# Weight sums and a running sum of squares: the same subtractions and additions on GpSimd instead of VectorE

## The chip, the cores and the metric

The kernel runs on one core of a Trainium2 chip. The core has a matrix engine (TensorE, PE in the profile, with its weight loads as PEld), a vector engine (VectorE, DVE), an activation engine (ScalarE, ACT), GpSimd (POOL) and SyncE (SP), which here issues the DMA transfers. Each engine works through its own instruction stream in order and waits at semaphores for the others. The metric is the device time of one execution in microseconds.

## The reference, cut to what matters

One layer of an encoder: 2048 tokens of width 1024, all in float32.

```
xn   = RMSNorm(x)
proj = xn @ w_in                      # attention q,k,v; mLSTM q,k,v,o and gates; ga, gm
A    = chunked band attention with a relative-position bias, 8 heads of 64
M    = mLSTM in chunks of 64, 4 heads of 128, with convolution, norm and output gate
y    = sigmoid(ga) * (A @ w_att_proj) + sigmoid(gm) * (M @ w_mlstm_proj)
x    = x + y @ w_out
x    = x + relu(RMSNorm(x) @ w_up)^2 @ w_down
out  = RMSNorm(x)
```

## The kernel before, in words

**Tiling.** Tokens are cut into four blocks of 512. Every float32 product is made of three TensorE passes in a rounded format (fp32r): each operand is split into a rounded upper part, which ScalarE copies, and the remainder, which VectorE subtracts (L427 and L429 for weights of 128x1024, L963 and L968 for activations of 128x512); then come high times high, high times low and low times high. A DMA puts raw weights into one of four buffers `wraw`, the split weights lie in one of three buffers `wsp`.

**Seven products for eight.** The output projection, both feed-forward matrices and the input projection of blocks 2 and 3 work on a matrix of two by two quarters with seven products instead of eight (`quad`, L571, and `quad_tok`, L599). This needs sums of quarters on both sides. For weights some sums are formed once ahead of time and kept in DRAM as `wsum` (`self.td`): `sum_w(q)` at L381 loads the four quarters of half a quad, 128x512 each, from `in_wf` into four buffers of the pool `ctx` (L391), forms `c-a`, `d-c`, `d-(c-a)` and `b-(d-(c-a))` in place (L396), and after each sends the result to DRAM (`store`, L2054). The third subtraction overwrites the first one's result, so it waits until that has been stored. Fourteen quads with two halves of four subtractions make 112. The loader later reads the sums as weights (L409, `wraw<-wsum`). Other sums are formed when the weights are first used (`quad_w`, L446).

The results of the seven products are put together by `combine`: ScalarE copies a bank to `ctx` (L1764), VectorE adds the next bank to it (L1772), and that sets the bank free for the next product.

**The squares.** `norm_mid` (L2059) needs, for the norm ahead of the feed-forward part, the sum of squares of the residual stream over the 1024 features of a block. `square_mid` (L2084) loads one of eight tiles of 128x512 into a buffer `sc`, ScalarE squares it (L2089), and for all but the first VectorE adds it to a running sum in a buffer `bias` (L2093). Four blocks with seven additions make 28. The result is needed much later, when the feed-forward output is added to the residual stream (`residual`, L2141).

**What sets the order.** The instruction streams are written by a planner (`Flow`, L95) when the program is built. Every piece of work is a thread that names an engine and an assumed duration (`yield "dve", dve_ns(512)`), waits for events and takes buffers from pools; `run` (L173) picks what can start first by its own clock, then by priority. Its choice fixes the order on each engine, on SP's queue of DMA issues, and which buffer is taken. The times assumed there are not those of the chip, and the chip follows only the order and the semaphores.

**Stages.** Up to about 640 us blocks 0 and 1 go through the input projection, attention and the recurrence. To about 1500 us follow gate and output products, the input products of blocks 2 and 3 (with most weight sums beside them) and the first up-projection. To about 2150 us the attention and recurrence of blocks 2 and 3 run beside the first down-projection; then comes the same tail for blocks 2 and 3.

Of the kernel before, what the change touches and what calls it, by code (L numbers as in the profile page):

```python
# [27 lines left out]
ALU = mybir.AluOpType  # L28
# [66 lines left out]
class Flow:  # L95
# [8 lines left out]
               dve=dict(pe=220.0, act=130.0, dve=130.0, pool=155.0), pool=dict(pe=290.0, act=130.0, dve=60.0),  # L104
# [107 lines left out]
def act_ns(n, ps=False, ap=0):  # L212
    return (51 if ps else 93) + 0.834 * n + 93 * ap


def dve_ns(n):
    return 70 + 1.042 * n
# [7 lines left out]
class Layer:  # L225
# [155 lines left out]
    def sum_w(self, q):  # L381

        fl, V = self.fl, self.nc.vector
        for h in range(2):
            got = yield "get", self.ctx, 4
            a, b, c, d = (x[:, :512] for x in got)
            wf, td = (t[:, :, h * 512:h * 512 + 512] for t in (self.io["wf"][q], self.td[q].ap()))
            kept = [Event() for _ in range(4)]
            for n, x in ((0, a), (1, c), (3, d), (2, b)):
                yield "sp", 900, 2000  # L390
                self.nc.sync.dma_start(x, wf[n])  # L391
            for n, dst, x, y in ((0, a, c, a), (2, c, d, c), (1, a, d, a), (3, b, b, a)):
                if n == 1:
                    yield "wait", [kept[0]]
                yield "dve", dve_ns(512)
                V.tensor_sub(dst, x, y)  # L396
                fl.spawn(self.store(td[n], dst, kept[n]), 1)
            yield "wait", kept
            fl.put(self.ctx, *got)
            fl.set(self.td_ev[q][h])  # L400
# [1683 lines left out]
    def square_mid(self, s, h, j, x, tot, summed):  # L2084
        x5 = x[0][:, :512]
        yield "sp", 900, 2000
        self.nc.sync.dma_start(x5, self.x2d[2 * s + h].ap()[j])
        yield "act", act_ns(512)
        self.nc.scalar.square(tot if j == 0 else x5, x5)  # L2089
        if j > 0:  # L2090
            yield "wait", [summed[j - 1]]
            yield "dve", dve_ns(512)
            self.nc.vector.tensor_add(tot, tot, x5)  # L2093
        self.fl.put(self.sc, x)
        self.fl.set(summed[j])

# [361 lines left out]
```

## Time and profile before

| | before |
|---|---|
| median of 3 runs | 2867.71 us (2861.02 to 2868.32) |
| span of the profiled execution | 2865.0 us |
| PE busy | 2815.4 us, 98% |
| DVE busy | 2037.9 us, 71% |
| ACT busy | 1558.1 us, 54% |
| POOL busy | 48.2 us, 2% |
| mean granted TensorE clock | 0.994 |

The profile lists no time of its own for the profiled execution beside its span, from the first instruction to the last; the span lies within the three times measured. A group's row names the line, the engine, what is written and read, the shape and the count; behind the bar come its total busy time, the mean of one in ns, the engine's idle time just ahead of it and what ended that. Waits are listed as "who waited <- for whom: us in total, times, longest". A row of the timeline gives the start, the duration, and in square brackets the idle time of that engine ahead of it and its releaser. A window's row gives the busy time of each engine in that stretch, with the number of instructions in brackets.

### The profile page before, as it was taken

The numbers are of one execution on the slowest core, as the hardware profiler recorded it, in microseconds if no ns is written. First come the engines' busy times: TensorE is split into PE (matmuls) and PEld (weight loads), VectorE is DVE, ScalarE is ACT, GpSimd is POOL, SyncE is SP. The second block draws the span as 40 slices with busy tenths as digits, with TensorE's granted clock in tenths as the row PEclk, the third lists the DMA queues.
The fourth block names the chain that finished last, engine by engine and source line by source line (L and its number), as shares of the span: only waits on it lengthen the run. The fifth ranks groups of instructions, "written<-read, shape, count | busy, mean of one in ns | idle before, by whom it ended". The sixth has DMA issues, their size and how long they took to land.

```text
span 2865.0 us, 39043 instructions
## 1 busy us (share of the span) xinstructions
PE 2815.4 (98%) x13576; PEld 2350.6 (82%) x13576; DVE 2037.9 (71%) x3783; ACT 1558.1 (54%) x2701; POOL 48.2 (2%) x116
## 2 busy tenths in 40 slices
PE   8999999999999999999999999999999999999998
PEld 7888888888878888877888888788778788888887
DVE  6886479778896867875666887778876744455565
ACT  4664366755444545664556666446644655554444
POOL 0000000000000000000000000000000000000000
PEclk9999999999999999999999999999999999999999
DMA  6327632357765768587878866577567655566563
GB/s 216 100 90 257 240 112 89 129 191 251 255 214 188 250 224 286 179 276 254 305 274 284 256 190 224 185 235 236 188 216 268 216 199 194 189 242 210 188 225 134
DMA packets 276005, 605.74 MB, mean 211 GB/s; under 512 B 30688, under 2 KB 45152, under 8 KB 275808
## 3 DMA queue, kind: packets, MB, share of 16 engines
q1 hardware_dynamic: 275808, 603.26, 62.6%
q8 instruction: 106, 1.74, 0.2%
q14 instruction: 91, 0.75, 0.1%
HBM read 426.98 MB, written 176.16 MB: 211 GB/s over the span
## 4 chain that ended last, share of the span: by engine, by line
PE 83%; DVE 7%; DMA 4%; ACT 3%; issue 1%; POOL 0%; SPq 0%; POOLq 0%; DVEq 0%; ACTq 0%
PE bank L571 36%; PE bank L488 12%; PE bank L489 12%; PE bank L490 12%; PE bank L599 2%; PE bank L1220 2%; PE bank L1255 2%; DMA r<-u 2%; PE bank L1286 1%; DVE wsp L429 1%; DVE r L968 1%; ACT wsp L427 1%; DVE sc L1261 1%; DVE r L1291 1%; DMA x<-ctx 1%
## 5 line engine op out<-in xcount | busy, mean ns | idle before, releaser
L571 PE MATMUL bank<-r,wsp 128*128 128x512 f32 x5208 | 1194.4, 391 | 9.4 <-DVE ctx L1772 7.2
L571 PEld LDWEIGHTS bank<-r,wsp 128*128 128x128 f32 x5208 | 980.0, 189 | 216.5 <-DVE ctx L1772 8.9
L429 DVE TENSOR_TENSOR wsp<-wraw,wsp 128x1024 fp32r<-128x1024 f32 x461 | 563.1, 1222 | 341.5 <-ACT wsp L427 299.0
L427 ACT CAST wsp<-wraw 128x1024 fp32r<-128x1024 f32 x461 | 484.2, 1051 | 493.7 <-PE bank L571 191.6
L488 PE MATMUL bank<-r,wsp 128*128 128x512 f32 x1600 | 640.7, 401 | 0.4 <-DVE ctx L1658 0.3
L490 PE MATMUL bank<-r,wsp 128*128 128x512 f32 x1600 | 625.2, 391 | 0.0
L489 PE MATMUL bank<-r,wsp 128*128 128x512 f32 x1600 | 624.8, 391 | 0.0
L490 PEld LDWEIGHTS bank<-r,wsp 128*128 128x128 f32 x1600 | 300.3, 188 | 64.6
L488 PEld LDWEIGHTS bank<-r,wsp 128*128 128x128 f32 x1600 | 301.1, 188 | 52.4 <-DVE ctx L1658 0.5
L489 PEld LDWEIGHTS bank<-r,wsp 128*128 128x128 f32 x1600 | 301.4, 188 | 51.7 <-DVE r L968 0.2
L1772 DVE TENSOR_TENSOR ctx<-bank,ctx 128x512 f32<-128x512 f32 x174 | 119.0, 687 | 85.2 <-PE bank L571 83.8
L963 ACT CAST r<-r 128x512 fp32r<-128x512 f32 x224 | 136.5, 622 | 78.0 <-DMA r<-u 74.2
L968 DVE TENSOR_TENSOR r<-r 128x512 fp32r<-128x512 f32 x224 | 149.7, 686 | 32.9 <-ACT r L963 31.8
L1270 ACT ACTIVATE sc<-sc,scs 128x640 f32<-128x640 f32 (+4 forms) x128 | 97.4, 761 | 77.1 <-DVE scs L1267 74.7
L1764 ACT COPY ctx<-bank 128x512 f32<-128x512 f32 x174 | 101.1, 582 | 66.7 <-PE bank L571 59.2
L396 DVE TENSOR_TENSOR ctx<-ctx,ctx 128x512 f32<-128x512 f32 x112 | 76.7, 688 | 73.5 <-DMA ctx<-in_wf 56.2
L2131 ACT ACTIVATE ctx<-ctx 128x512 f32<-128x512 f32 x96 | 60.6, 631 | 106.1 <-DVE ctx L1772 106.0
L1261 DVE CUSTOM_DVE_ANT_0 sc<-bank,bias 128x320 f32<-128x320 f32 (+3 forms) x240 | 104.6, 459 | 19.3 <-PE bank L1255 15.6
L1220 PE MATMUL bank<-r,r 128*128 128x256 f32 (+1 forms) x672 | 112.8, 288 | 5.6 <-DVE r L1291 3.6
L1220 PEld LDWEIGHTS bank<-r,r 128*128 128x128 f32 x672 | 100.4, 194 | 19.7 <-DVE r L1291 9.3
L1291 DVE TENSOR_TENSOR r<-bank,r 128x512 fp32r<-128x512 f32 (+1 forms) x168 | 96.9, 594 | 10.7 <-ACT r L1289 9.8
L1289 ACT CAST r<-bank 128x512 fp32r<-128x512 f32 (+1 forms) x168 | 81.8, 516 | 17.4 <-PE bank L1286 13.1
(275 smaller groups left out, 2884.9 us busy)
## 6 DMA issues: line engine op xcount, KB each, us to landing
wraw<-in_wf SPq DMA_DIRECT2D x170, 512.0 KB, 4.2
wraw<-wsum SPq DMA_DIRECT2D x136, 512.0 KB, 3.9
r<-u SPq DMA_DIRECT2D x224, 256.0 KB, 3.8
wraw<-in_w SPq DMA_DIRECT2D x104, 512.0 KB, 3.8
u<-ctx SPq DMA_DIRECT2D x128, 256.0 KB, 2.5
ctx<-in_wf SPq DMA_DIRECT2D x112, 256.0 KB, 4.3
wsum<-ctx SPq DMA_DIRECT2D x112, 256.0 KB, 3.6
u<-tmp SPq DMA_DIRECT2D x96, 256.0 KB, 2.9
```

Of the source, the lines that this page charges most:

```text
L427: nc.scalar.copy(w[:, 0], raw)
L429: nc.vector.tensor_sub(w[:, 1], raw, w[:, 0].bitcast(F32))
L488: mm(ps, lh, rh, start=first, stop=False)
L489: mm(ps, lh, rl, start=False, stop=False)
L490: mm(ps, ll, rh, start=False, stop=last)
L571: mm(ps, wv[:, x, k, n], a[:, y], start=new and k == 0 and x == y == 0, stop=k == 3 and x == 1, skip_group_check=True)
L963: self.nc.scalar.copy(dst[:, 0], src)
L968: self.nc.vector.tensor_sub(dst[:, 1], src, dst[:, 0].bitcast(F32))
L1220: nc.tensor.matmul(bk[:, c0:c0 + w], st, sl[:, x, o:o + w], start=n == 0, stop=n == total - 1)
L1261: nc.vector.tensor_tensor_reduce(out=e[:, x * w:x * w + w], in0=bks[x][:, :w], in1=br[:, j0 + x * w:j0 + x * w + w], op0=ALU.add, op1=ALU. ...
L1291: nc.vector.tensor_sub(slot[:, 1, :o], bk[:, :o], slot[:, 0, :o].bitcast(F32))
L1772: nc.vector.tensor_add(t[:, o:o + 512], ps, t[:, o:o + 512])
```

## The change

Both operations keep their operands, their place in the threads and their results. They are issued to GpSimd, and the planner is told so, with an assumed 1450 ns in place of VectorE's 70 + 1.042 x 512 = 604 ns.

```diff
@@ sum_w
             for n, dst, x, y in ((0, a, c, a), (2, c, d, c), (1, a, d, a), (3, b, b, a)):
                 if n == 1:
                     yield "wait", [kept[0]]
-                yield "dve", dve_ns(512)
-                V.tensor_sub(dst, x, y)
+                yield "pool", 1450
+                self.nc.gpsimd.tensor_tensor(dst, x, y, op=ALU.subtract)
                 fl.spawn(self.store(td[n], dst, kept[n]), 1)
@@ square_mid
         if j > 0:
             yield "wait", [summed[j - 1]]
-            yield "dve", dve_ns(512)
-            self.nc.vector.tensor_add(tot, tot, x5)
+            yield "pool", 1450
+            self.nc.gpsimd.tensor_tensor(tot, tot, x5, op=ALU.add)
```

## Prediction

> **What bounds the kernel now.** I read the page first, then what TensorE and VectorE waited for, then stretches of the timeline around TensorE's gaps.
>
> ```profile
> span 2865.0 us, 39043 instructions
> ...
> PE 2815.4 (98%) x13576; PEld 2350.6 (82%) x13576; DVE 2037.9 (71%) x3783; ACT 1558.1 (54%) x2701; POOL 48.2 (2%) x116
> ...
> L396 DVE TENSOR_TENSOR ctx<-ctx,ctx 128x512 f32<-128x512 f32 x112 | 76.7, 688 | 73.5 <-DMA ctx<-in_wf 56.2
> ...
> wsum<-ctx SPq DMA_DIRECT2D x112, 256.0 KB, 3.6
> ```
>
> TensorE is the bound: of 2865.0 us only 2865.0 - 2815.4 = 49.6 us are idle. Whatever the change does to VectorE's 71%, it can gain no more than what of these 49.6 us it removes. So the question is which gaps of TensorE end on the moved work.
>
> ```profile
> PE bank L571 <- DVE ctx L1772: 7.2, 4, 3.5
> PE bank L1286 <- DVE sc L1274: 6.4, 3, 2.9
> ...
> PE bank L599 <- DVE ctx L1772: 1.2, 2, 0.8
> ```
>
> No gap ends on L396 or L2093 themselves. But 7.2 + 1.2 = 8.4 us end on L1772, the addition that sets a PSUM bank free, and L1772 stands behind L396 in VectorE's order. What VectorE waits for, and TensorE's rows around those gaps:
>
> ```profile
> DVE ctx L396 <- DMA ctx<-in_wf: 56.2, 30, 5.9
> ...
> DVE ctx L396 <- DMA wsum<-ctx: 16.4, 11, 3.1
> ...
> DVE bias L2093 <- ACT sc L2089: 6.0, 6, 1.4
> ```
>
> ```profile
> 993.63 1.29 DVE L396 TENSOR_TENSOR ctx<-ctx,ctx 128x512 f32<-128x512 f32 x2
> 996.81 1.40 PE L599 MATMUL bank<-wsp,r 128*128 128x512 f32 x5 [0.84 <-DVE ctx L1772]
> 1108.70 0.69 DVE L396 TENSOR_TENSOR ctx<-ctx,ctx 128x512 f32<-128x512 f32 x1 [0.48 <-DMA ctx<-in_wf]
> 1111.69 1.62 PE L599 MATMUL bank<-wsp,r 128*128 128x512 f32 x6 [0.38 <-DVE ctx L1772]
> 1227.94 2.33 PE L571 MATMUL bank<-r,wsp 128*128 128x512 f32 x9 [1.75 <-DVE ctx L1772]
> 1266.97 3.02 PE L571 MATMUL bank<-r,wsp 128*128 128x512 f32 x12 [0.65 <-DVE ctx L1772]
> 1269.89 0.69 DVE L396 TENSOR_TENSOR ctx<-ctx,ctx 128x512 f32<-128x512 f32 x1 [2.98 <-DMA ctx<-in_wf]
> 1271.24 0.96 PE L571 MATMUL bank<-r,wsp 128*128 128x512 f32 x3 [1.26 <-DVE ctx L1772]
> 1305.36 1.42 DVE L396 TENSOR_TENSOR ctx<-ctx,ctx 128x512 f32<-128x512 f32 x2 [5.89 <-DMA ctx<-in_wf]
> 1306.69 0.68 DVE L1772 TENSOR_TENSOR ctx<-bank,ctx 128x512 f32<-128x512 f32 x1
> 1309.68 0.68 DVE L1772 TENSOR_TENSOR ctx<-bank,ctx 128x512 f32<-128x512 f32 x1
> 1310.42 2.08 PE L571 MATMUL bank<-r,wsp 128*128 128x512 f32 x4 [3.53 <-DVE ctx L1772]
> ```
>
> The pattern is plainest at 1305: VectorE stands 5.89 us at a subtraction whose operand has not landed, the additions behind it run late, and TensorE idles 3.53 us. The waits of 72.6 us (56.2 + 16.4) are mostly swallowed by spare banks: a stall of 2.98 us cost 1.26, one of 5.89 cost 3.53. So TensorE forgives a VectorE stall of about 1.7 to 2.4 us.
>
> **The change part by part.**
>
> *Removed from VectorE: L396 and its waits.* 112 x 688 ns = 76.7 us of work and 72.6 us of waiting. On TensorE's path I count the gaps with an L396 stall or an L396 pair right ahead: 3.53 + 1.26 + 0.84 + 0.38 = 6.0 us. The 0.65 at 1266.97 may add to it; the 1.75 at 1227.94 has no L396 close ahead of it and is left. Ends: 0 (the two long stalls could be replaced by others) and 8.4. I take 6.0. Late next at those places is L429 or L1772 itself, waiting for ScalarE or for the bank.
>
> *Removed from VectorE: L2093.*
>
> ```profile
> L2093 DVE TENSOR_TENSOR bias<-bias,sc 128x512 f32<-128x512 f32 x28 | 19.2, 688 | 6.4 <-ACT sc L2089 6.0
> ```
>
> 28 x 688 ns = 19.2 us and 6.0 us of waits. In none of TensorE's gaps does it stand ahead. Its result is used at the end of the feed-forward products, hundreds of us later, which hides the longer chain too; with that cover gone, seven additions of some 1.2 instead of 0.69 us would cost about 3.6 us a block. I take 0.
>
> *Added to GpSimd: 140 subtractions and additions of 128x512 with two inputs.* No such row exists. The nearest are GpSimd's one-input operation of that size and VectorE at those moments.
>
> ```profile
> L1544 POOL TENSOR_SCALAR ctx<-ctx,ghead x8: 697/1158/2187, 99.1 to 546.1; 128x512 f32<-128x512 f32 x8
> ...
> 181.37 0.70 POOL L1544 TENSOR_SCALAR ctx<-ctx,ghead 128x512 f32<-128x512 f32 x1
> ```
>
> ```profile
> 403.62 1.21 DVE L429 TENSOR_TENSOR wsp<-wraw,wsp 128x1024 fp32r<-128x1024 f32 x1
> 404.17 1.22 POOL L1544 TENSOR_SCALAR ctx<-ctx,ghead 128x512 f32<-128x512 f32 x1 [9.78 <-ACT ctx L1541]
> 405.04 0.70 DVE L1274 TENSOR_SCALAR sc<-sc,scs 128x640 f32<-128x640 f32 x1
> ...
> L1274 DVE TENSOR_SCALAR sc<-sc,scs 128x640 f32<-128x640 f32 x96 | 52.8, 551 | 1.1
> ...
> 498.17 2.19 POOL L1544 TENSOR_SCALAR ctx<-ctx,ghead 128x512 f32<-128x512 f32 x1 [12.22 <-ACT ctx L1541]
> 498.66 1.22 DVE L429 TENSOR_TENSOR wsp<-wraw,wsp 128x1024 fp32r<-128x1024 f32 x1
> ```
>
> Alone it takes 0.70 us. At 404.17 it ends 0.56 us after L429 does (405.39 against 404.83), at 498.17 0.48 us after (500.36 against 499.88): GpSimd stood while VectorE ran a subtraction with both inputs in SBUF. And L1274, at 405.04, took 0.70 against a mean of 0.551: VectorE waited too. The engines exclude each other. With two inputs I estimate between 0.70 (as one input) and 1.40 (twice it), 1.2 as the value nearer to two reads, and up to 2.2 with the wait for VectorE. GpSimd grows by about 140 x 1.5 = 210 us and stays far from a bound.
>
> The Trainium skill, "GPSIMD Engine Reference", Performance versus the Vector engine, gives 4497 ns for a two-input float32 addition of 2048 elements; a quarter of it is 1.12 us, an estimate from that page. The same skill, "SBUF — State Buffer", Who interferes with whom, says that a VectorE instruction with two SBUF inputs and a GpSimd instruction that reads SBUF hold a shared port one after the other, the later one fully blocked; the rows at 404 and 498 agree.
>
> What VectorE gives back: at the least 0.15 us x 140 = 21 us (as L1274), at the most the whole 1.2 x 140 = 168 us, more than the 95.9 us removed. I take about a third of the most, 56 us, since operations that read a bank (L1772) showed no such wait: VectorE nets some 40 us. On TensorE's path each block of up to 1.2 us lies under the 1.7 us that it forgives, so I take 0; ends -3 (VectorE is earlier elsewhere) and +20 (below).
>
> *Stores and SP.* The 112 stores wait on GpSimd instead of VectorE, each some 0.5 to 1.5 us later, and what is behind them in SP's order waits as well, weight loads among it.
>
> ```profile
> SPq L409 <- DVE wsp L429: 663.8, 237, 10.0
> ...
> SPq L2054 <- DVE ctx L396: 65.2, 53, 5.8
> ```
>
> With 53 waits longer by 0.8 us the 65.2 become about 108 us. Against it, SP spends 663.8 us standing until a `wraw` buffer is free, so weights are fetched as soon as there is room: 0 on the path. If that cover failed, a weight tile late by 1 us stops TensorE 1 us. Each sum also holds its four `ctx` buffers about 3 us longer (four by 0.8); taken at 0 for the same reason.
>
> *GpSimd's queue.* L1618 (the norm of a recurrence head), L850 and the mask fills L1149/L1150 now stand behind moved work that waits for DMAs. In the changed order few do: one L396 ahead of the last L1618 of block 0, eight ahead of L850, a group ahead of the first fills of blocks 2 and 3. Between 0 and 3 us; I take 0, since L850's predecessor on VectorE stood behind the same subtractions.
>
> *The planner's new order.* With other durations the planner also reorders work that isn't edited: TensorE's stream differs in the attention of block 1 and in that of blocks 2 and 3, and is the same again from about 2150 us.
>
> ```profile
> 1500.00:2150.00 650.00, 630.89 (x3368) 536.19 (x3367) 513.78 (x1194) 373.43 (x753) 15.69 (x45) 0.99 0.70 223
> ```
>
> TensorE idles 650.00 - 630.89 = 19.1 us in that stretch, on softmax steps too close to their scores. Counting the matmuls of 128x512 size between the last scores of a tile and its first transpose, the closest six in the order before stand 6 to 15 apart, the closest five in the new one 1 to 20. Neither is better on its face: 0, with half of 19.1 either way as the ends.
>
> *Sum.* 2865.0 - 6.0 = 2859.0 us of span. The span is 2.7 us below the median of the runs shown, so on the median's scale 2867.7 - 6.0 = 2861.7.
>
> **The rivals.**
>
> *Port blocking makes it slower.* Place: the dense stretch of sums around 1220 to 1490.
>
> ```profile
> 1220.00:1320.00 100.00, 92.81 (x394) 75.29 (x393) 67.48 (x93) 58.31 (x90) 0.00 (x0) 0.97 0.83 283
> ```
>
> VectorE is busy 67.48 of 100 us there, so it isn't full, and one block is forgiven; two in a row (2.4 us) ahead of L1772 are not. If half of about 40 sums cost TensorE 1 us each: +20 - 6 = +14, 2882 us. It decides once the gaps ending on L1772 pass today's 8.4 us. For it: both engines visibly wait for each other. Against: most of those L396 stood still on DMAs anyway.
>
> The Trainium skill's rule on the shared port ("SBUF — State Buffer", Who interferes with whom) would favour this rival; no row here has it with a two-input GpSimd operation.
>
> *The new order costs attention.* Half of 19.1 more: 2867.7 - 6.0 + 9.5 = 2871 us. *The new order and a freer VectorE help attention.* Half of it less: 2867.7 - 6.0 - 9.5 = 2852 us. For both only that the streams differ there.
>
> **How the numbers follow.** Forecast, 2861.7 us with its own range of 2855 to 2867: 0.43. Port blocking, 2882: 0.22. Attention worse, 2871: 0.15. Attention better, 2852: 0.20. 0.3% of 2867.7 is 8.6 us, about what a measurement of this kernel can tell from no change. Faster, below 2859.1: nine tenths of the last case and two fifths of the forecast, 0.18 + 0.17, about 0.36. Slower, above 2876.3: most of port blocking and a third of attention worse, 0.19 + 0.05 = 0.24. Same: 0.40. The range for 8 in 10 reaches from 2846, a little below the better attention, to 2884, a little above port blocking.
>
> **What would show it.** Right: no wait of VectorE on `in_wf` or `wsum<-ctx` at L396; gaps of TensorE ending on L1772 down from 8.4 to about 2 us; VectorE's busy time near 1942 us (2037.9 - 95.9) plus what blocking stretches; GpSimd's moved rows at 1.2 to 2.2 us. Wrong: gaps on L1772 or on L427 grow between 1220 and 1490, SP's waits for L396 go far above 108 us, GpSimd rows above 2.2 us, or the stretch from 1500 to 2150 changes its 19.1 us by more than half.

## The result, and the profile after

| | before | after |
|---|---|---|
| median (5 runs each) | 2864.18 us (2861.02 to 2868.32) | 2886.76 us (2885.60 to 2891.28) |
| span of the profiled execution | 2865.0 us | 2884.6 us |
| DVE busy | 2037.9 us | 2021.2 us |
| POOL busy | 48.2 us | 272.9 us |
| TensorE's gaps ending on L1772 | 8.4 us | 7.7 us |

The changed kernel takes 1.0077 times as long, with an interval of 1.0064 to 1.0090: it is slower by about 22 us, where 6 us less were forecast, and lies 2.8 us above the range.

The page of the changed kernel, with the rows that answer to those shown of before:

```profile
span 2884.6 us, 39126 instructions
...
PE 2818.9 (98%) x13576; PEld 2346.8 (81%) x13576; DVE 2021.2 (70%) x3644; ACT 1551.6 (54%) x2700; POOL 272.9 (9%) x256
...
L429 DVE TENSOR_TENSOR wsp<-wraw,wsp 128x1024 fp32r<-128x1024 f32 x461 | 583.2, 1266 | 403.6 <-ACT wsp L427 389.5
...
L396 POOL TENSOR_TENSOR ctx<-ctx,ctx 128x512 f32<-128x512 f32 x112 | 181.3, 1623 | 773.1 <-DMA ctx<-in_wf 696.0
```

VectorE lost 95.9 us of work but only 2037.9 - 2021.2 = 16.7 us of busy time. The other 79.2 us (2021.2 - 1942.0) went into operations that were not edited and now last longer: 0.57 us for each moved operation. L429, a split of weights, is the largest of them: 1266 ns in the mean instead of 1222, as the page of before has it:

```profile
L429 DVE TENSOR_TENSOR wsp<-wraw,wsp 128x1024 fp32r<-128x1024 f32 x461 | 563.1, 1222 | 341.5 <-ACT wsp L427 299.0
```

GpSimd is busy 9% of the span, far from a bound, and still TensorE's idle time rose from 49.6 to 2884.6 - 2818.9 = 65.7 us. What TensorE and SP waited for:

```profile
PE bank L571 <- DVE ctx L2015: 7.2, 3, 5.9
PE bank L571 <- DVE r L968: 6.7, 2, 6.2
PE bank L571 <- DVE ctx L1772: 6.1, 6, 2.5
...
PE bank L599 <- DVE ctx L1772: 1.6, 2, 1.3
```

```profile
SPq L2054 <- POOL ctx L396: 155.0, 80, 7.9
```

Behind a wait of 7.6 us on L427 that the kernel before has as well (7.5), two new gaps of about 6 us stand at the head: one ends on L968, the split of an activation operand, one on L2015, an addition that reads a bank of the output projection and so sets it free. To find where the 19.6 us of span arose, compare the same stretches of both traces. First before, then after; the first number behind the comma is the stretch's length, the next TensorE's busy time with its matmuls, and the third column from the right the granted clock.

```profile
780.00:900.00 120.00, 119.71 (x533) 95.35 (x532) 102.24 (x159) 57.92 (x88) 0.00 (x0) 1.00 0.60 206
1200.00:1500.00 300.00, 292.81 (x1286) 241.06 (x1285) 201.12 (x265) 165.99 (x248) 0.69 (x5) 0.99 0.80 276
1500.00:2200.00 700.00, 680.89 (x3592) 577.62 (x3591) 541.50 (x1231) 392.25 (x778) 16.57 (x45) 0.99 0.71 228
2200.00:2300.00 100.00, 98.09 (x426) 80.74 (x425) 77.01 (x108) 68.68 (x107) 0.00 (x0) 0.98 0.60 204
```

```profile
780.00:900.00 120.00, 109.19 (x466) 84.58 (x465) 97.50 (x124) 52.67 (x81) 43.16 (x27) 0.96 0.55 183
1200.00:1500.00 300.00, 296.92 (x1317) 245.18 (x1316) 199.07 (x220) 170.85 (x255) 82.93 (x55) 1.00 0.80 278
1500.00:2200.00 700.00, 679.99 (x3591) 574.78 (x3590) 539.90 (x1237) 387.57 (x778) 17.39 (x47) 0.99 0.73 228
2200.00:2300.00 100.00, 92.99 (x400) 75.93 (x399) 78.28 (x92) 65.39 (x102) 22.61 (x14) 0.97 0.67 219
```

Every stretch has the same length, so matmuls that are missing are lag; turned into time by the mean of the stretch this is an estimate, since the matmuls of a stretch are not all alike. From 780 to 900 us the changed kernel issues 67 matmuls fewer; at 120 / 533 = 0.225 us each that is 15.1 us. From 1200 to 1500 it gains 31, or 7.2 us. From 2200 to 2300 it loses 26, or 6.1 us. The attention of blocks 2 and 3 (1500 to 2200) is unchanged. With 25 matmuls lost ahead of 780 and between 900 and 1200 us (3.2 and 2.1 us in the same way) this makes 19 of the 19.6 us.

The loss at 780 to 900 is where `take_parts` (L1726, L1741) and `take_split` (L963, L968) form the activation operands of the next products one after the other, all but L963 on VectorE. The timeline there, before and then after:

```profile
808.25 1.90 DVE L968 TENSOR_TENSOR r<-ctx,r 128x512 fp32r<-128x512 f32 x3
...
810.06 1.41 DVE L1726 SCALAR_TENSOR_TENSOR tmp<-tmp,gcol,bias 128x512 f32<-128x512 f32 x2
811.39 0.69 DVE L968 TENSOR_TENSOR r<-tmp,r 128x512 fp32r<-128x512 f32 x1
```

```profile
812.54 8.42 POOL L2093 TENSOR_TENSOR bias<-bias,sc 128x512 f32<-128x512 f32 x5 [1.81 <-ACT bias L2089]
813.01 5.17 DVE L968 TENSOR_TENSOR r<-ctx,r 128x512 fp32r<-128x512 f32 x3
...
818.10 3.42 DVE L1726 SCALAR_TENSOR_TENSOR tmp<-tmp,gcol,bias 128x512 f32<-128x512 f32 x2
820.93 5.10 POOL L396 TENSOR_TENSOR ctx<-ctx,ctx 128x512 f32<-128x512 f32 x3
821.44 1.75 DVE L968 TENSOR_TENSOR r<-tmp,r 128x512 fp32r<-128x512 f32 x1
...
823.25 2.08 PE L571 MATMUL bank<-r,wsp 128*128 128x512 f32 x4 [6.20 <-DVE r L968]
```

Three splits that took 1.90 us take 5.17, two L1726 take 3.42 instead of 1.41, and GpSimd's five additions take 8.42 us, 1.68 each. The engines take turns here: each VectorE instruction stands for about one instruction of GpSimd, the next GpSimd instruction for one of VectorE, and so on through the row, at about 1.7 us each. A chain that took 3.83 us up to the end of its L968 (808.25 to 812.08) took 10.18 (813.01 to 823.19), and TensorE stood 6.20 us. By duration (minimum, median, maximum in ns) two lines of VectorE in the changed kernel:

```profile
L968 DVE TENSOR_TENSOR r<-ctx,r x81: 674/685/1795, 42.2 to 2270.1; 128x512 fp32r<-128x512 f32 x81
...
L1772 DVE TENSOR_TENSOR ctx<-bank,ctx x174: 674/688/693, 659.1 to 2552.2; 128x512 f32<-128x512 f32 x174
```

L968 reads two operands from SBUF and reaches 1795 ns. L1772 reads one of its two from a PSUM bank and never passes 693, as in the trace of before. That is the rule of the Trainium skill, "SBUF — State Buffer", Who interferes with whom, by which a VectorE instruction with two SBUF inputs contends with a GpSimd instruction that reads SBUF and one with a single SBUF input, outside the 2-port performance modes, does not; this trace agrees, 1795 against 693 ns.

### The profile page after: what moved, and what is told of

It is laid out like the page before. It is cut to its first block, busy times and chain, and to the rows that moved or that the text cites. A ratio compares the mean times of both kernels' runs of the same rounds, so it can differ in the third digit from the quotient of the medians.

```text
span 2884.6 us, 39126 instructions
## 1 busy us (share of the span) xinstructions
PE 2818.9 (98%) x13576; PEld 2346.8 (81%) x13576; DVE 2021.2 (70%) x3644; ACT 1551.6 (54%) x2700; POOL 272.9 (9%) x256
## 4 chain that ended last, share of the span: by engine, by line
PE 71%; DVE 14%; DMA 6%; issue 5%; ACT 4%; POOL 1%; SPq 0%; POOLq 0%; DVEq 0%; ACTq 0%
PE bank L571 31%; PE bank L488 10%; PE bank L489 10%; PE bank L490 10%; DVE wsp L429 2%; PE bank L599 2%; DVE r L968 2%; PE bank L1220 2%; DMA r<-u 1%; PE bank L1255 1%; PE bank L1286 1%; ACT wsp L427 1%; DVE r L970 1%; DVE r L1291 1%; DVE sc L1261 1%
## 5 line engine op out<-in xcount | busy, mean ns | idle before, releaser
L429 DVE TENSOR_TENSOR wsp<-wraw,wsp 128x1024 fp32r<-128x1024 f32 x461 | 583.2, 1266 | 403.6 <-ACT wsp L427 389.5
L427 ACT CAST wsp<-wraw 128x1024 fp32r<-128x1024 f32 x461 | 484.1, 1050 | 493.1 <-PE bank L489 193.0
L396 POOL TENSOR_TENSOR ctx<-ctx,ctx 128x512 f32<-128x512 f32 x112 | 181.3, 1623 | 773.1 <-DMA ctx<-in_wf 696.0
L1772 DVE TENSOR_TENSOR ctx<-bank,ctx 128x512 f32<-128x512 f32 x174 | 118.6, 687 | 100.7 <-PE bank L571 100.7
L963 ACT CAST r<-r 128x512 fp32r<-128x512 f32 x224 | 135.8, 623 | 68.8 <-DMA r<-u 61.4
L968 DVE TENSOR_TENSOR r<-r 128x512 fp32r<-128x512 f32 x224 | 149.1, 687 | 30.1 <-ACT r L963 28.8
L446 DVE TENSOR_TENSOR wraw<-wraw,wraw 128x1024 f32<-128x1024 f32 x68 | 91.0, 1340 | 15.6 <-DMA wraw<-in_wf 12.7
```

What stands on the lines that cost most here:

```text
L396: self.nc.gpsimd.tensor_tensor(dst, x, y, op=ALU.subtract)
L427: nc.scalar.copy(w[:, 0], raw)
L429: nc.vector.tensor_sub(w[:, 1], raw, w[:, 0].bitcast(F32))
L963: self.nc.scalar.copy(dst[:, 0], src)
L968: self.nc.vector.tensor_sub(dst[:, 1], src, dst[:, 0].bitcast(F32))
```

## The experiments

Each diff is against the changed kernel, unless it says otherwise. Ratios are to the kernel before, measured beside each run (its medians there were 2865.94, 2866.34 and 2870.27 us), with their intervals.

**One half alone.** The first kernel moves only the weight sums, the second only the squares.

```diff
@@ square_mid (sums only)
-            yield "pool", 1450
-            self.nc.gpsimd.tensor_tensor(tot, tot, x5, op=ALU.add)
+            yield "dve", dve_ns(512)
+            self.nc.vector.tensor_add(tot, tot, x5)
@@ sum_w (squares only)
-                yield "pool", 1450
-                self.nc.gpsimd.tensor_tensor(dst, x, y, op=ALU.subtract)
+                yield "dve", dve_ns(512)
+                V.tensor_sub(dst, x, y)
```

> Only the weight sums (L396) go to GpSimd; the squares' sums (L2093) stay on VectorE. Port theory (GpSimd holds VectorE's second SBUF input, and the loss comes where the back-to-back L2093 stand beside the forming of activation operands): the TensorE gaps of 6.2 us near 823 and 5.9 us near 2244 go, the relief between 1200 and 1400 of some 7 us stays; 0.2% to 0.4% faster than before, about 2857 us. Order theory (the loss comes from the planner's new order): the order is new here too, so slower than before by something like 0.3 to 0.8%.

> Only the squares' sums (L2093, 28 operations) go to GpSimd. Port theory: most of the loss is here, 0.5 to 0.9% slower than before (15 to 25 us), with L968 and L1741 at 1.6 to 1.8 us instead of 0.69 beside it. Order theory: no telling, near before if this plan differs little. If the weight sums were the cause, the same as before.

Measured: sums only 2883.94 us, 1.0063 (1.0048 to 1.0078); squares only 2889.35 us, 1.0078 (1.0063 to 1.0093). Each half costs nearly as much as both. The squares cost as much as the port theory said. The sums do not: it forecast 0.2% to 0.4% faster, and 0.63% slower lies in the range of the order theory, which only the next pair of kernels rules out. The halves overlap in one place: at 780 to 900 us the sums alone lose 533 - 474 = 59 matmuls, the squares alone 533 - 495 = 38, both together 67.

The squares alone stretch VectorE, as above:

```profile
807.01 8.43 POOL L2093 TENSOR_TENSOR bias<-bias,sc 128x512 f32<-128x512 f32 x5 [211.19 <-ACT bias L2089]
807.47 5.18 DVE L968 TENSOR_TENSOR r<-ctx,r 128x512 fp32r<-128x512 f32 x3
...
816.65 2.07 PE L571 MATMUL bank<-r,wsp 128*128 128x512 f32 x4 [4.98 <-DVE r L968]
```

Where the squares run, this kernel loses 38 + 14 matmuls, about 12 us (8.6 + 3.3). Part of that may again be waits for buffers: between 800 and 860 us SP stood 14.6 us, 10.0 of it at once, until GpSimd's L2093 gave back an `sc` buffer to load. As large a loss is in a stretch where none of the 28 moved additions runs:

```profile
1500.00:2200.00 700.00, 673.09 (x3543) 568.01 (x3542) 539.43 (x1229) 384.63 (x771) 16.12 (x46) 0.99 0.71 223
```

That is 3592 - 3543 = 49 matmuls fewer than before, or 9.5 us, where the changed kernel loses one matmul. The planner gives the squares alone an order of their own. That this share comes from the order is likely, but not shown, since no run has that order without the move.

The sums alone show a second path, through SP. In their timeline four subtractions on GpSimd last 11.05 us. They share that time with VectorE's L446 and L429, and not in turns throughout: the first subtraction takes 4.79 us, while two L446 and an L2093 run at their usual length.

```profile
826.19 11.05 POOL L396 TENSOR_TENSOR ctx<-ctx,ctx 128x512 f32<-128x512 f32 x4 [5.66 <-DMA ctx<-in_wf]
...
826.88 2.35 DVE L446 TENSOR_TENSOR wraw<-wraw,wraw 128x1024 f32<-128x1024 f32 x2
...
831.01 2.63 SPq L2054 DMA_DIRECT2D wsum<-ctx  x2
...
835.98 1.83 SPq L404 DMA_DIRECT2D wraw<-in_wf  x4
840.54 1.04 ACT L427 CAST wsp<-wraw 128x1024 fp32r<-128x1024 f32 x1 [8.71 <-DMA wraw<-in_wf]
...
845.32 5.03 PE L571 MATMUL bank<-r,wsp 128*128 128x512 f32 x11 [5.14 <-DVE ctx L1772]
```

SP issues in order. It stood 7.8 us at the store of such a sum, up to 831.01, most of it through that long subtraction; the four weight loads of L404 behind it went out at 835.98, ScalarE then waited 8.71 us for the first of them, and TensorE 5.14.

**The planner's order by itself, and the move by itself.** The third kernel keeps the changed kernel's planner entries and issues both operations on VectorE. The fourth keeps the entries of before, and so its order, and issues them on GpSimd.

```diff
@@ new plan, VectorE
                 yield "pool", 1450
-                self.nc.gpsimd.tensor_tensor(dst, x, y, op=ALU.subtract)
+                V.tensor_sub(dst, x, y)
...
             yield "pool", 1450
-            self.nc.gpsimd.tensor_tensor(tot, tot, x5, op=ALU.add)
+            self.nc.vector.tensor_add(tot, tot, x5)
@@ old plan, GpSimd
-                yield "pool", 1450
+                yield "dve", dve_ns(512)
                 self.nc.gpsimd.tensor_tensor(dst, x, y, op=ALU.subtract)
...
-            yield "pool", 1450
+            yield "dve", dve_ns(512)
             self.nc.gpsimd.tensor_tensor(tot, tot, x5, op=ALU.add)
```

> The changed kernel's plan (the planner still counts on GpSimd and 1450 ns, so every other instruction stands as in the changed kernel), but the 140 operations are issued to VectorE at their place in that plan. Port theory: no stretched operations, so within 0.3% of before, VectorE's waits at L396 for DMAs back. Order theory: as slow as the changed kernel, 0.6 to 0.9% slower than before.

> The plan of before, with the 140 operations issued to GpSimd at their place in it. Port theory: slower than before by 0.4 to 1.0%, VectorE's busy time stretched by some 80 us as in the changed kernel. Order theory: 0.2 to 0.3% faster than before, since the order of everything else is that of before and the waits for DMAs leave VectorE.

Measured: the new order on VectorE 2862.66 us, 0.9991 (0.9982 to 1.0001); the old order on GpSimd 2894.11 us, 1.0095 (1.0078 to 1.0112). The new order doesn't cost the time; the engine does, with the new order (1.0077 against 0.9991) and with the old one (1.0095 against 1).

The new order on VectorE is also the clean comparison for the stretches above, since its order is the changed kernel's. From 780 to 900 us it issues 530 matmuls against 466, from 2200 to 2300 us 415 against 400: the move itself costs about 14.4 and 3.5 us there. From 1200 to 1500 us, with 1320 against 1317, it costs almost nothing.

The pair also corrects the reading of the gain at 1200 to 1500 us. There TensorE's gaps that end on L1772 come to 7.2 us before, 3.1 in the changed kernel, 2.6 with the new order on VectorE, and 13.8 with the old order on GpSimd. The relief is the new order's, which shows it without the move; in the old order the move makes this stretch worse, 1244 matmuls against 1286. Taking the subtraction off VectorE uncovered other waits there. Of two places, one had been the 3.53 us gap of before: VectorE no longer stands at the subtraction, but then at L446 for a weight tile (6.55 us) whose load went out late, and TensorE's gap grows to 4.71 us. At the other place the load stood behind a store for L396, at which SP waited 6.2 us until 1438.24, the longest of 70.0 us in that stretch (before 34.9):

```profile
1438.24 2.57 SPq L2054 DMA_DIRECT2D wsum<-ctx  x2
...
1443.38 1.71 SPq L404 DMA_DIRECT2D wraw<-in_wf  x1
...
1448.73 1.23 DVE L446 TENSOR_TENSOR wraw<-wraw,wraw 128x1024 f32<-128x1024 f32 x1 [6.59 <-DMA wraw<-in_wf]
...
1449.88 0.68 DVE L1772 TENSOR_TENSOR ctx<-bank,ctx 128x512 f32<-128x512 f32 x1
...
1450.61 1.65 PE L571 MATMUL bank<-r,wsp 128*128 128x512 f32 x3 [4.47 <-DVE ctx L1772]
```

**The same GpSimd time without the reads.** Each moved operation becomes three fills of 128x512 on GpSimd, which read nothing. The sums and the running sum themselves are left out of this kernel.

```diff
-                self.nc.gpsimd.tensor_tensor(dst, x, y, op=ALU.subtract)
+                other = y if x is dst else x
+                for t in (other if n != 3 else dst, dst, dst):
+                    self.nc.gpsimd.memset(t, 0.0)
...
-            self.nc.gpsimd.tensor_tensor(tot, tot, x5, op=ALU.add)
+            for t in (x5, tot, tot):
+                self.nc.gpsimd.memset(t, 1.0)
```

> The changed kernel's plan and places, but each of the 140 GpSimd operations is replaced by three fills of 128x512 (on its operand and twice on its result), which write but read nothing from SBUF; the sums are left out, so the output is not the reference's. About the same 1.3 to 1.5 us of GpSimd each. Port theory (GpSimd's reads hold VectorE's second SBUF input): VectorE's operations are no longer stretched, L429 at most 1.23 us and L968 at most 0.70, and the time falls back to that of the same plan on VectorE, 2855 to 2866 us. Lateness theory (the loss comes from GpSimd's results and stores being some 0.7 us later, whatever its port does): stays 0.5 to 0.8% slower than before.

Measured: 2870.54 us, 1.0012 (0.9998 to 1.0026). A fill takes 524 ns, three 1.57 us, close to the 1.62 of a sum, so results come about as late as in the changed kernel. But no VectorE row is stretched (L429 is L431 here, L968 is L970):

```profile
L431 DVE TENSOR_TENSOR wsp<-wraw,wsp x461: 1201/1224/1228, 7.5 to 2845.2; 128x1024 fp32r<-128x1024 f32 x154
```

The time lies between the two theories of the expectation. As an estimate, of the 0.77% some -0.09% is the order, about 0.2% the later results (1.0012 against 0.9991), and some 0.65% (1.0077 against 1.0012) comes with the reads. Each term is a difference of two ratios that are themselves known to within 0.10 to 0.14%, and the last one includes the waits of GpSimd itself and what they delay behind SP.

For the stretch from 780 to 900 us the split is not settled. The execution that was profiled took 2876.55 us, above its own median, and lost 533 - 477 = 56 matmuls there, against 67 in the changed kernel, with no VectorE row stretched:

```profile
780.00:900.00 120.00, 112.28 (x477) 87.59 (x476) 83.11 (x124) 54.09 (x83) 42.37 (x86) 0.96 0.60 197
```

ScalarE waited 23.3 us there for loads of `x` (6.7 before, 8.7 in the changed kernel), so late results alone can cost much of what is lost in this stretch. The gain of that execution over the changed kernel lies elsewhere: 1335 matmuls against 1317 from 1200 to 1500 us, 419 against 400 from 2200 to 2300.

**Which sums.** The late group is the 80 subtractions of the quads that are summed from about 947 us on, the early group the other 32. Each kernel moves one group and leaves the other, and the squares, on VectorE.

```diff
-                yield "pool", 1450
-                self.nc.gpsimd.tensor_tensor(dst, x, y, op=ALU.subtract)
+                if q in (2, 3, Q_VM, Q_VM + 1):        # the early kernel: not in
+                    yield "dve", dve_ns(512)
+                    V.tensor_sub(dst, x, y)
+                else:
+                    yield "pool", 1450
+                    self.nc.gpsimd.tensor_tensor(dst, x, y, op=ALU.subtract)
...
# and in square_mid, in both kernels, VectorE and dve_ns(512) as before
```

> GpSimd forms only the ten quads of weight sums that come after about 1000 us (80 of the 112 subtractions); the sums of the output projection and of the value columns and all squares' sums stay on VectorE. Port theory: beside the forming of activation operands GpSimd is then idle, so the 13 us lost between 800 and 900 in the run with all sums go; the waits for DMAs between 1200 and 1400 go too: 0.1 to 0.4% faster than before, 2855 to 2863 us. If contention costs the same everywhere: 0.3 to 0.5% slower.

> The counterpart of the run with the 80 later subtractions on GpSimd (which was level with before): only the 32 earlier ones, of the output projection's and the value columns' sums, are formed by GpSimd. Theory that the place decides (beside the forming of activation operands, near 820 to 850 us): 0.3 to 0.65% slower than before, with 8 to 14 us of TensorE's time lost between 800 and 900. Theory that the cost goes with the number: 0.63% x 32/112 = 0.2% slower.

Measured: the 80 late ones 2866.64 us, 1.0000 (0.9989 to 1.0012); the 32 early ones 2880.42 us, 1.0041 (1.0027 to 1.0055). The late ones stretch VectorE by 39.4 us (2022.3 instead of 2037.9 - 80 x 0.688 = 1982.9), 0.49 us for each, and in sum it costs nothing, where the port theory had forecast 0.1 to 0.4% faster. That sum hides two parts: the kernel issues 30 matmuls more than before from 1200 to 1500 us and about 30 fewer elsewhere. Both kernels have orders of their own, which no run shows without the move.

Fewer than half as many, at another place, cost 0.41%, as the theory of the place had forecast. The execution of the early group that was profiled, at 2888.26 us, was the slowest of five; it lost 533 - 469 = 64 matmuls, 14.4 us, from 780 to 900 us. SP again holds back a weight load there (the first row is of 800 to 870 us; L404 is L408 here, and the other lines that the rows name are four higher too):

```profile
SPq L2058 <- POOL ctx L400: 33.3, 11, 10.1
```

```profile
837.09 1.98 SPq L408 DMA_DIRECT2D wraw<-in_wf  x4
842.71 1.04 ACT L431 CAST wsp<-wraw 128x1024 fp32r<-128x1024 f32 x1 [12.35 <-DMA wraw<-in_wf]
...
847.50 2.90 PE L575 MATMUL bank<-r,wsp 128*128 128x512 f32 x6 [8.93 <-DVE ctx L1776]
```

**GpSimd reads that nothing needs.** The kernel before, with 28 additions on GpSimd behind the squares: each doubles a squared tile in place after VectorE has used it, and no result is read. Against before:

```diff
             self.nc.vector.tensor_add(tot, tot, x5)
+            self.nc.gpsimd.tensor_tensor(x5, x5, x5, op=ALU.add)
```

> The kernel before, all work on VectorE as it was, plus 28 GpSimd additions of 128x512 that no one needs: after each L2093 GpSimd doubles the squared tile in place. Port theory: VectorE's operations with two SBUF inputs beside them stretch by about 1.1 us each and TensorE loses part of what it lost with the squares moved, 0.15 to 0.5% slower (4 to 15 us), though no one waits for these results except the next load of the buffer. Lateness theory: no difference, below 0.1%.

Measured: 2877.82 us, 1.0042 (1.0029 to 1.0055). Here L2093 is on VectorE and the order is that of before; 37.5 us of GpSimd work stretched VectorE by 2055.1 - 2037.9 = 17.2 us and the kernel by about 12. Of the 17.2 us, 10.6 are L2093 itself (29.8 us instead of 19.2). Ahead of a gap of 5.80 us, three of them in a row take 1.49 us each instead of 0.69:

```profile
2266.06 4.48 DVE L2093 TENSOR_TENSOR bias<-bias,sc 128x512 f32<-128x512 f32 x3
...
2274.00 2.50 PE L571 MATMUL bank<-r,wsp 128*128 128x512 f32 x5 [5.80 <-DVE ctx L1772]
```

The additions also hold each `sc` buffer longer before its reload: between 2200 and 2290 us SP stood 15.2 us for GpSimd at those loads, where before it stood 6.4 us for VectorE's L2093. So this run shows the reads and the later buffers together, not the reads all alone. No result of GpSimd is waited for by VectorE or TensorE.

**Two that did not settle their question.** One kernel gives the sums' stores to GpSimd's own queue, so that SP never stands for them (against the kernel with the sums alone). The other is the kernel before with the loads of the sums assumed to take 4500 ns instead of 2000, which moves the subtractions later in VectorE's order.

```diff
@@ own queue
-                fl.spawn(self.store(td[n], dst, kept[n]), 1)
+                fl.spawn(self.store(td[n], dst, kept[n], eng=self.nc.gpsimd), 1)
@@ load price, against before
-                yield "sp", 900, 2000
+                yield "sp", 900, 4500
```

> As the run with only the weight sums on GpSimd, but the 112 stores of the sums are issued by GpSimd itself instead of SP, so that SP's queue no longer stands at them. The run with SP's stores was 0.63% slower than before, and beside its largest gap (5.3 us near 845) SP stood 7.8 us at such a store with four weight loads behind it. If SP's queue carries a large part of the loss: 0.2 to 0.4% slower than before. If the port alone carries it: still 0.55 to 0.75% slower, or more, for what GpSimd's issuing costs.

> The kernel before with one number of the plan changed: the loads of the quarters for the weight sums are taken to land 4.5 us after their issue instead of 2.0 (the profile has a median of 4.3). All on VectorE. Theory that the waits of 72.6 us at L396 cost TensorE some 6 us: those waits fall below 30 us and the time by 3 to 7 us, 0.1 to 0.25%. Rival: the new order costs as much elsewhere, no difference.

Measured: own queue 2922.14 us, 1.0176 (1.0161 to 1.0191), far above the 0.55 to 0.75% of its expectation, which allowed for more only by what GpSimd's issuing costs; load price 2872.85 us, 1.0027 (1.0014 to 1.0040). The first can't tell SP's share, since GpSimd pays for each store itself: 112 issues of 557 ns (62.3 us in all), and a subtraction that lasts up to 7.39 us. The second cut the waits of L396 for `in_wf` from 56.2 to 38.9 us and with those for `wsum<-ctx` the waits at L396 from 72.6 to 59.6, not below 30 as its expectation asked. It was 0.27% slower, with another order as well, so it doesn't tell what a shorter wait on VectorE is worth.

No version beats the kernel before: the two best, the new order on VectorE and the late sums, have intervals that include 1.

## Why the prediction was wrong, step by step

*Removing L396 from VectorE, -6.0 us: wrong.* VectorE no longer waits at L396, as forecast, and the gaps at 1200 to 1500 us shrank from 7.2 to 3.1 us. But the runs give this to the new order (2.6 us with L396 still on VectorE), while the move in the old order brought 13.8. At 1305 us the wait for the operand was real, but a second wait, for a weight tile, stood behind it and left a gap of 4.71 us instead of 3.53. That those subtractions stand ahead of the gaps in VectorE's order was taken for their cause. Over the whole kernel the gaps ending on L1772 went from 8.4 to 7.7 us, not to 2.

*Removing L2093, 0 us: wrong.* The squares alone cost 0.78%. The step asked whether L2093 stands ahead of a gap and whether its result is needed late. Both answers were right. What it left out is what runs beside it: the forming of operands at 807 and 2225 us, where that kernel loses about 12 of its 22 us, waits for `sc` buffers included. Some 9.5 us more were lost from 1500 to 2200 us, where no moved operation runs, and that share stays open.

*GpSimd's durations, 1.2 us (0.70 to 1.40, up to 2.2): about right.* The minimum is 1283 ns for L396 and 1268 for L2093, the medians 1416 and 1600, the maxima 2482 and 2603; together 225.9 us (181.3 + 44.6) against 210.

*What VectorE gives back, 56 us (21 to 168): right in kind, 79.2 measured.* The step that failed is its effect on TensorE: "On TensorE's path each block of up to 1.2 us lies under the 1.7 us that it forgives, so I take 0". A block is about 1.1 us, but blocks do not come alone. At 813 us, where both engines had a row of work, six VectorE instructions in a chain were blocked and lost 10.18 - 3.83 = 6.35 us, far above the 1.7 us that TensorE was to forgive: its gap was 6.20 us, and another, at L2015, 5.9. The end of +20 that was kept for this is about the size that came, about 22 us, though SP's share is in that as well.

*Stores and SP, 0 us: wrong.* The waits of SP for L396 are 155.0 us instead of about 108, in 80 times. The cover that was named, 663.8 us of SP's standing for free `wraw` buffers, is a total over the kernel; at 826 to 847 us the weight loads were due, and 7.8 us of standing with the sums alone, 10.1 with the early sums alone, passed on to TensorE as 5.14 and 8.93 us. In the changed kernel itself it was less: SP stood at most 4.1 us for L396 between 800 and 860 us, and the gap there is 2.52 us.

*GpSimd's queue, 0 us:* not tested by itself; none of the gaps above hangs on it.

*The new order, 0 us: right in sum,* 0.9991, with the attention stretch idle 20.0 us against 19.1. It was not neutral in detail, as the gain at 1200 to 1500 us shows.

*The rivals.* Port blocking was the right mechanism, and its 2882 us the nearest figure. That the figure is so near is in part luck, because its place, 1220 to 1490, was not the one: with the same order the move costs almost nothing there (1317 matmuls against 1320), and the loss is at 780 to 900 and 2200 to 2300 us. With the old order the gaps there do pass the 8.4 us at which it was to decide (13.8), but those examined end on L446's waits for weight tiles, not on two blocks in a row ahead of L1772. Both attention rivals are out. The forecast's own signs spoke as written: SP's waits far above 108 us and GpSimd rows above 2.2 us were named as signs of an error.

## What to carry to other kernels

The price of an operation moved to GpSimd is not set by GpSimd's idle time but by what VectorE does beside it: look up in the timeline which VectorE instructions with two SBUF operands run at that moment, and whether TensorE is waiting for a chain of them. Then look at what waits for the slower result: what stands behind its store in the DMA queue, and which loads need the buffers that it holds. When a change also gives a planner new durations, run the new order with the old engines before crediting a gap to the move.

## What the runs showed of the hardware that was not expected

- With work waiting on both, VectorE and GpSimd alternated one for one at 813 to 826 us of the changed kernel: VectorE's 0.68 us became up to 1.79, GpSimd's 1.27 about 1.7. That is no rule for every place: with the sums alone one GpSimd subtraction lasted 4.79 us while three VectorE instructions ran ahead of it.
- Fills on GpSimd, which only write, left VectorE's instructions with two SBUF operands at their old length (1228 ns at most). The Trainium skill, "SBUF — State Buffer", Who interferes with whom, says so too: the contention is with a GpSimd instruction that reads SBUF, not with one that only writes it.
- These gaps cost TensorE more than their idle time. After the gap of 6.20 us the granted clock of the changed kernel was 0.50 for the next 4 us, after the one of 2.52 us it was 0.68 for 5.3 us:

```profile
823.00:827.00 4.00, 3.29 (x7) 1.90 (x8) 4.00 (x4) 1.59 (x3) 2.95 (x2) 0.50 0.37 142
850.99:856.30 5.31, 5.31 (x16) 4.22 (x17) 2.71 (x3) 2.68 (x4) 2.79 (x2) 0.68 0.56 211
```

From 780 to 900 us the idle time grew by 119.71 - 109.19 = 10.5 us, the lag by 15.1; the rest is the 466 matmuls at 109.19 / 466 = 0.234 us instead of 119.71 / 533 = 0.225, with a mean clock of 0.96 instead of 1.00.
